# The wide products of two feed-forwards and a short convolution: high weights against both token parts in one matmul

## The chip, the cores and the metric

The kernel runs on one core of a Trainium2 chip. The metric is the device time of one launch in microseconds; the profile's span is counted from the first to the last instruction of one such execution, inside that time. An engine's name in a row is PE (TensorE matmul), PEld (TensorE weight load), DVE (VectorE), ACT (ScalarE), POOL (GpSimd) or SP (SyncE, whose queue issues the loads).

## The reference

One token block of 256 rows and 1024 columns goes through a feed-forward, a token mixing (retention and neighbourhood attention), a second feed-forward, a recurrent mixer and a short-convolution mixer, all in float32. The stages that matter here:

```python
def _swiglu(x, w_in, w_out):                      # w_in 1024 x 5632, w_out 2816 x 1024
    g, u = jnp.split(x @ w_in, 2, axis=-1)
    return (jax.nn.silu(g) * u) @ w_out

def shortconv_mixer(h, w_in, conv_w, w_out):      # w_in 1024 x 6144, w_out 1536 x 1024
    u = jnp.einsum('bsd,dc->bsc', h, w_in)
    bg, cg = u[..., :WIDTH], u[..., WIDTH:2 * WIDTH]
    xv, gate = u[..., 2 * WIDTH:3 * WIDTH], u[..., 3 * WIDTH:]
    y = bg * causal_depthwise_conv(cg * xv, conv_w)
    return jnp.einsum('bsc,cd->bsd', y * jax.nn.silu(gate), w_out)
```

Each stage begins with an RMS norm of the running sum `x` and ends by adding its result to it.

## The kernel before, in words

**Products.** A float32 product is made of three matmuls in fp32r. Weights and tokens are each split in a high part (a rounded copy, by ACT, L94 for weights) and a low part (the rest, by DVE, L96); `mm3` (L240 to L244) passes high by high (L242), low by high (L243 or L244 by the operands' order) and high by low. The third low by low is dropped.

**Weights.** All weights come in parts of 128 x 1024 in one order, through the class `Stream`. A ring of 41 slots of 128 x 1024 (`RING`, L23) holds raw parts, their high and low halves, and the token pairs. `load` issues a part's DMA on SP's queue, `split` makes its halves, `use` (called at a part's first use) keeps the split up to 15 parts ahead as far as free slots less `S.reserve` allow, and `done` gives two slots back. So how far the weights run ahead is set by the ring.

**Token pairs.** `Pair` holds the transposed tokens: `h` and `l` tiles of four blocks of 128 x 256 each, in the ring. `transpose_pair` (L366 to L378) turns 128 x 128 blocks on PE (L372) and writes high by ACT (L376), low by DVE (L377).

**Stage one, `phase_a`** (from L431): columns of the weights come out on the partitions, tokens on the free side. The first unit or two of each stage are done per token half (`mm_tok`, tokens stationary, 512 weight columns moving). They begin before the second half of the tokens is there: `nxt.ready(1)` turns it in between. All other units, 256 weight columns and two parts each, go through `mm_a2`: for each 128 columns `m` and each of 8 blocks `k`, three matmuls with the weights stationary and 256 token columns moving (L242 high weights by high tokens, L243 high weights by low tokens, L244 low weights by high tokens), into half a PSUM bank. There are 8 banks, given out in rotation. In `ffn` the eviction `evac` (L499 to L509) holds the bank of the gate, and at the second of two units does silu on ACT (L505), the product on DVE (L506) and `split_pair` (L483, L484). In `shortconv` four units are held, then copied, multiplied, convolved and split (L1095 to L1106).

**Stage two, `phase_b`** (from L391): tokens stationary, 512 weight columns moving, two banks for each token half. The last 8 parts are passed first for one token half, so that the norm of this half runs while PE passes the other.

**The joint** between a stage two and the next stage one is where PE can run short: norm, transposes and weight splits share ACT and DVE. While a stage two runs, `S.reserve` is 4, so that the next token pair finds its slots; it is set to 0 once the pair is there.

The instructions of each engine are ordered by a scheduler which the program runs through when it is built; each engine then takes its own in order.

Of the kernel before, what the change touches and what calls it, by code (L numbers as in the profile page):

```python
# [19 lines left out]
RD = 128  # L20
NH, ND = 8, 64
EPS = 1e-6
RING = 41  # L23
RAW_AHEAD = 4
AHEAD = 15
RATE = 3
# [24 lines left out]
class Stream:  # L51
# [80 lines left out]
def block_kernel(ctx: ExitStack, tc: tile.TileContext, A, C, out):  # L132
# [4 lines left out]
    const = ctx.enter_context(tc.tile_pool(name="const", bufs=1))  # L137
    gp = ctx.enter_context(tc.tile_pool(name="gains", bufs=2))
    wp = ctx.enter_context(tc.tile_pool(name="work", bufs=2))
    tp = ctx.enter_context(tc.tile_pool(name="tmp", bufs=6))  # L140
# [60 lines left out]
    u_ax = ax  # L201
# [30 lines left out]
    one = const.tile([128, 128], F32, name="one")  # L232
    dve.memset(one, 1.0)
    S.ahead = 6
    S.load(4)
# [10 lines left out]
    class Pair:  # L246
# [27 lines left out]
        def drop(self):  # L274
            self.used(self.nk - 1)

    def mm_a2(bk, u, xt):

        for m in range(2):
            c = slice(m * 128, (m + 1) * 128)  # L280
            for q, p in enumerate(u.parts):
                if m == 0:
                    S.use(p)
                for j in range(p.a):
                    k = q * p.a + j
                    mm3(bk[:, m * SEQ:(m + 1) * SEQ], (p.hi[:, j, c], p.lo[:, j, c]), xt.at(k),
                        k == 0, k == u.a - 1)
                if m == 1:
                    S.done(p)

    def mm_tok(ps, u, q, xt, t):

# [87 lines left out]
    class Next:  # L380
# [5 lines left out]

        def ready(self, t):
            if self.pair is None:
                self.pair = Pair(NKD)
            S.hold = transpose_pair(self.hn[t], t, self.pair, 0, NKD)  # L390

    def phase_b(us, xt, post_ap, halved, next_ap, late, last=False):


        acc = [columns(0, 512, D), columns(0, 512, 768, D) if last else columns(0, 512, D)]
        ps = [p for u in us for p in u.parts]
        n, late = len(ps), 2 * late
        S.reserve = 4
        nxt = Next()
        for k, p in enumerate(ps[:n - late]):  # L400
            S.use(p)
            for t in range(2):
                mm_b(acc[t], p, xt, t, k, n)
            S.done(p)
            xt.used(k)
        post = gain(post_ap) if post_ap is not None else None
        pre = gain(next_ap)


        order = []  # L410
        for t in range(2):
            order += [(t, k, acc[t]) for k in range(n - late, n - 4)]
            order += [(t, k, [a]) for a in acc[t] for k in range(n - 4, n)]
        for q, (t, k, a) in enumerate(order):
            p = ps[k]
            if q == len(order) - 6 and not last:
                nxt.ready(0)
                S.reserve = 0
            if a[0] is acc[t][0]:
                S.use(p, 1 if t == 0 or last or nxt.pair else 0)  # L420
            mm_b(a, p, xt, t, k, n)
# [9 lines left out]
    def phase_a(tok, us, nxt, evac, tok_evac, lead):  # L431

# [27 lines left out]
                turned()  # L460
            turned = tok_evac(i, b)
        for i, u in enumerate(us):
            b = bank()
            mm_a2(b, u, xt)
            if turned:
                turned()
                turned = None
            evac(i, b)
# [25 lines left out]
    def ffn(us, nxt, post, next_ap, lead, aside=None):  # L494
        f = Pair(NKF)
        held = {}
        done = 2 * len(us[0])

        def evac(i, b):  # L499
            if i % 2 == 0:  # L500
                held[i] = b
                return
            g = held.pop(i - 1)
            sg = tmp()
            act.activation(out=sg, in_=g, func=AF.Silu)  # L505
            dve.tensor_tensor(out=sg, in0=sg, in1=b, op=ALU.mult)  # L506
            split_pair(f, done + i - 1, 2, two(sg))
            if done + i == 15 and aside:
                aside()  # L509
# [9 lines left out]
        xt = phase_a(us[0], us[1], nxt, evac, tok_evac, lead)  # L519
        xt.drop()  # L520
        return phase_b(us[2], f, post, True, next_ap, LATE_B)


# [30 lines left out]
    def mixing(nxt):  # L554
# [62 lines left out]


        nqk = [S.slot(F32, "nqk") for _ in range(2)]

        def full_a(u, xt):
            b = bank()
            mm_a2(b, u, xt)
            return b

        for i, u in enumerate(u_nq + u_nk):
            b = full_a(u, xt)
# [211 lines left out]
        for i, u in enumerate(u_gn + u_gr):  # L839
# [11 lines left out]
            elif i < 6:  # L851
                transpose_pair(yn[i - 4], i - 4, zt, 0, NKD)
                S.drop()
        xt.drop()


        for i, u in enumerate(u_no):
# [30 lines left out]
    vec_b = const.tile([128, 36], F32, name="vec_b")  # L888
    cneg = const.tile([128, 24], F32, name="cneg")

    def channel_vectors():
        r = tmp()
# [4 lines left out]
        S.fetch(r[0:36, 128:256], A["b_conv_w_2"].rearrange("k (h p) -> (k h) p", p=128))  # L897
        ps = bank()
        pe.transpose(ps[:, 0:96], r[0:96, 0:128], ident[0:96, 0:96])
        pe.transpose(ps[:, 96:132], r[0:36, 128:256], ident[0:36, 0:36])  # L900
# [12 lines left out]
    def recurrent(nxt):  # L913
# [139 lines left out]
                S.drop()  # L1053

        banks = []
        xt = phase_a(u_at, u_ax, nxt, evac, tok_evac, 1)

        for j, u in enumerate(u_ag):
            b = bank()
# [5 lines left out]
        xt.drop()  # L1065
        S.aside()
        for j in range(EARLY, 6):
            finish(j)
# [3 lines left out]
    def shortconv(nxt):  # L1072
# [21 lines left out]

        def evac(i, b):  # L1095
            held.append(b)
            if i % 4 != 3:
                return
            cg, xv, bg, gt = held
            held.clear()  # L1100
            w = tmp()
            act.activation(out=w, in_=cg, func=AF.Copy)
            dve.tensor_tensor(out=w, in0=w, in1=xv, op=ALU.mult)
            sg = tmp()
            act.activation(out=sg, in_=gt, func=AF.Silu)
            convolved(1 + i // 4, w, (bg, sg))  # L1106

        def tok_evac(i, b):
            w = tmp()
# [14 lines left out]
                    convolved(0, a, (g,))  # L1124
            return turned

        xt = phase_a(u_bt, u_b, nxt, evac, tok_evac, 2)
        xt.drop()
        return phase_b(u_bo, y, None, False, A["final_g_2"], LATE_B, last=True)


    LATE_B, LATE_O = 4, 3

    def prepare():
        S.fetch(rot, C["rot"])
        S.fetch(mask, C["mask"])
        decay_logs()
        channel_vectors()

    first = Next()  # L1140

# [76 lines left out]
```

## Time and profile before

| what | us |
| --- | --- |
| median of 3 runs | 922.97 (922.52 to 924.29) |
| the profiled execution: its own time | 922.03 |
| its span | 920.2 |
| PE busy in the span | 908.0 (99%) |
| DVE busy | 564.4 (61%) |
| ACT busy | 471.3 (51%) |

A matmul's busy time in a row is longer than the distance to the next one, since matmuls are pipelined and their ends are modelled. What a matmul costs is therefore read as the distance from one start to the next. Busy shares of ACT and DVE are averages over the stages; for a stage the windows are read.

### The profile page before, as it was taken

What the parts mean: (1) busy time and instruction counts of PE and PEld (TensorE: products, weight loads), DVE (VectorE), ACT (ScalarE), POOL (GpSimd) and SP (SyncE); (2) the same over time, 40 slices, a digit from 0 to 9 for tenths busy, and PEclk for the clock granted to TensorE, in tenths of its full rate; (3) what the DMA queues carried; (4) which work ended last, traced back from release to release, by engine and by line L of the source; (5) the groups of instructions that cost most, each with busy time, mean ns of one, the idle gap of its engine ahead of it and who ended that gap; (6) DMA issues with size and microseconds to landing.
All of it is one profiled execution on the core that took longest, in us unless ns stands there. A gap on an engine that the chain in (4) does not pass through costs nothing.

```text
span 920.2 us, 15017 instructions
## 1 busy us (share of the span) xinstructions
PE 908.0 (99%) x6082; PEld 836.0 (91%) x6082; DVE 564.4 (61%) x743; ACT 471.3 (51%) x672; POOL 13.1 (1%) x24
## 2 busy tenths in 40 slices
PE   8999999999999999999999999999999999999997
PEld 5999998888978899998899999888998879999986
DVE  6954646358945454666874446526787977656523
ACT  7844545335755454534664444515869755444412
POOL 0000000000000000000000000000000000000000
PEclk9999999999999999999999999999999999999999
DMA  9965547748536353667565546756525757555401
GB/s 292 348 209 161 174 164 251 251 107 243 179 115 227 118 174 115 215 184 243 166 209 160 162 160 205 240 191 206 186 93 191 245 159 252 184 160 184 161 1 46
DMA packets 132811, 168.67 MB, mean 183 GB/s; under 512 B 12545, under 2 KB 112645, under 8 KB 132742
## 3 DMA queue, kind: packets, MB, share of 16 engines
q1 hardware_dynamic: 132308, 167.11, 56.9%
q8 instruction: 48, 0.79, 0.3%
q10 hardware_dynamic: 434, 0.59, 0.2%
q14 instruction: 21, 0.17, 0.1%
HBM read 166.64 MB, written 1.05 MB: 182 GB/s over the span
## 4 chain that ended last, share of the span: by engine, by line
PE 90%; ACT 4%; DVE 3%; DMA 1%; issue 1%; SPq 0%; POOL 0%; POOLq 0%; DVEq 0%; ACTq 0%
PE bank L242 29%; PE bank L243 28%; PE bank L244 28%; PE bank L372 1%; DVE lo L96 1%; DVE ri L1045 1%; PE bank L754 1%; PE bank L779 1%; ACT hi L94 1%; DMA raw<-in_b_w_in 1%; ACT ri L982 1%; ACT u L981 1%; PE bank L664 0%; ACT ri L960 0%; DMA x<-in_x 0%
## 5 line engine op out<-in xcount | busy, mean ns | idle before, releaser
L96 DVE TENSOR_TENSOR lo<-raw,hi 128x1024 fp32r<-128x1024 f32 (+1 forms) x304 | 360.1, 1209 | 137.1 <-ACT hi L94 75.2
L242 PE MATMUL bank<-ph,hi 128*128 128x256 f32 x1360 | 387.3, 285 | 0.0
L94 ACT ACTIVATE hi<-raw 128x1024 fp32r<-128x1024 f32 (+1 forms) x304 | 308.1, 1044 | 152.5 <-PE bank L244 72.8
L243 PE MATMUL bank<-pl,hi 128*128 128x256 f32 x1360 | 385.0, 283 | 0.0
L244 PE MATMUL bank<-ph,lo 128*128 128x256 f32 x1360 | 385.0, 283 | 0.0
L243 PEld LDWEIGHTS bank<-pl,hi 128*128 128x128 f32 x1360 | 261.0, 192 | 0.4
L242 PEld LDWEIGHTS bank<-ph,hi 128*128 128x128 f32 x1360 | 261.0, 192 | 0.3
L244 PEld LDWEIGHTS bank<-ph,lo 128*128 128x128 f32 x1360 | 261.0, 192 | 0.1
L242 PE MATMUL bank<-hi,ph 128*128 128x512 f32 (+1 forms) x540 | 208.8, 387 | 1.1 <-ACT ph L376 1.1
L243 PE MATMUL bank<-lo,ph 128*128 128x512 f32 (+1 forms) x540 | 206.5, 383 | 0.0
L244 PE MATMUL bank<-hi,pl 128*128 128x512 f32 (+1 forms) x540 | 205.2, 383 | 0.1
L242 PEld LDWEIGHTS bank<-hi,ph 128*128 128x128 f32 x540 | 101.9, 189 | 23.5 <-ACT ph L376 3.2
L244 PEld LDWEIGHTS bank<-hi,pl 128*128 128x128 f32 x540 | 101.7, 189 | 20.4 <-DVE pl L377 0.8
L243 PEld LDWEIGHTS bank<-lo,ph 128*128 128x128 f32 x540 | 102.0, 189 | 19.6 <-DVE lo L96 0.6
L483 ACT ACTIVATE ph<-tmp 128x512 fp32r<-128x512 f32 x28 | 17.6, 629 | 60.2 <-DVE tmp L506 48.7
L327 ACT ACTIVATE tmp<-x 128x512 f32<-128x512 f32 (+1 forms) x25 | 15.4, 614 | 39.8 <-DVE x L352 31.1
L506 DVE TENSOR_TENSOR tmp<-tmp,bank 128x512 f32<-128x512 f32 x19 | 13.0, 685 | 30.8 <-PE bank L244 30.8
L360 DVE TENSOR_TENSOR tmp<-bank,g 128x512 f32<-128x512 f32 x12 | 8.3, 692 | 36.0 <-ACT tmp L357 35.7
L357 ACT ACTIVATE tmp<-bank 128x512 f32<-128x512 f32 x12 | 7.2, 599 | 42.7 <-PE bank L244 42.4
L484 DVE TENSOR_TENSOR pl<-tmp,ph 128x512 fp32r<-128x512 f32 x28 | 19.1, 690 | 11.8 <-ACT ph L483 11.8
L377 DVE TENSOR_TENSOR pl<-bank,ph 128x512 fp32r<-128x512 f32 x24 | 16.0, 686 | 14.2 <-ACT ph L376 14.2
L319 POOL TENSOR_TENSOR small<-small,half 128x1 f32<-128x1 f32 x18 | 10.8, 601 | 802.2 <-DVE small L317 802.2
(146 smaller groups left out, 432.9 us busy)
## 6 DMA issues: line engine op xcount, KB each, us to landing
raw<-in_ffn_w_in SPq DMA_DIRECT2D x76, 512.0 KB, 5.2
raw<-in_w_mix_in SPq DMA_DIRECT2D x52, 512.0 KB, 4.0
raw<-in_ffn_w_out SPq DMA_DIRECT2D x44, 512.0 KB, 4.0
raw<-in_b_w_in SPq DMA_DIRECT2D x40, 512.0 KB, 4.6
raw<-in_a_w_in SPq DMA_DIRECT2D x20, 512.0 KB, 6.1
raw<-in_a_w_out SPq DMA_DIRECT2D x12, 512.0 KB, 4.4
raw<-in_b_w_out SPq DMA_DIRECT2D x12, 512.0 KB, 4.4
raw<-in_w_ret_out SPq DMA_DIRECT2D x8, 512.0 KB, 4.9
```

The lines of the kernel that those rows point to most:

```text
L94: self.copied = self.nc.scalar.activation(out=p.hi, in_=p.raw, func=AF.Copy)
L96: self.nc.vector.tensor_tensor(out=p.lo, in0=p.raw, in1=p.hi.bitcast(F32), op=ALU.subtract)
L242: pe.matmul(ps, a[0], b[0], start=first, stop=False)
L243: pe.matmul(ps, a[0], b[1], start=False, stop=False)
L244: pe.matmul(ps, a[1], b[0], start=False, stop=last)
L319: nc.gpsimd.tensor_tensor(out=r, in0=v, in1=half[:, 0:1], op=ALU.pow)
L327: sq = act.activation(out=tmp()[:, :c1 - c0], in_=x[:, t, c0:c1], func=AF.Square, scale=1.0 / 32, accum_out=ss[:, c:c + 1])
L372: pe.transpose(ps[:, j * 128:(j + 1) * 128], src[:, (b + j) * 128:(b + j + 1) * 128], ident)
L377: d = dve.tensor_tensor(out=lo, in0=pv, in1=h.bitcast(F32), op=ALU.subtract)
L483: act.activation(out=h, in_=src, func=AF.Copy)
L484: dve.tensor_tensor(out=lo, in0=src, in1=h.bitcast(F32), op=ALU.subtract)
L506: dve.tensor_tensor(out=sg, in0=sg, in1=b, op=ALU.mult)
```

## The change

The units of `phase_a` in both feed-forwards and in the short convolution (20, 18 and 20 units; not the units per token half, and none of the mixing or of the recurrent mixer) go through `wide` in place of `mm_a2`. The stage's tokens lie in a tile `xt` in which the high and the low part of a block stand side by side (`both(k)`: 512 columns). For each 128 weight columns, eight matmuls pass the high weights by these 512 columns into a whole bank; eight more pass the low weights by the 256 high columns into the first half of it. The bank is then summed into a tile in SBUF: ACT copies its second half, DVE adds the first.

```diff
-RING = 41
+RING = 37
...
+    xp = ctx.enter_context(tc.tile_pool(name="xt", bufs=1))
+    tp = ctx.enter_context(tc.tile_pool(name="tmp", bufs=7))
...
+    class Wide:
+        def __init__(self):
+            self.t = xp.tile([128, NKD, 2, SEQ], F32R, tag="x", name="xt")
...
+    def mm_a2w(bs, u, xt, after):
+        for m, b in enumerate(bs):
+            c = slice(m * 128, (m + 1) * 128)
+            for z in range(2):
+                for q, p in enumerate(u.parts):
+                    if m == z == 0:
+                        S.use(p)
+                    for j in range(p.a):
+                        k = q * p.a + j
+                        if z == 0:
+                            pe.matmul(b, p.hi[:, j, c], xt.both(k), start=k == 0, stop=False,
+                                      skip_group_check=True)
+                        else:
+                            pe.matmul(b[:, 0:SEQ], p.lo[:, j, c], xt.at(k)[0], start=False,
+                                      stop=k == u.a - 1, skip_group_check=True)
+                    if m == z == 1:
+                        S.done(p)
+            after(m, b)
+
+    def wide(u, xt, out):
+        def summed(m, b):
+            o = out[:, m * SEQ:(m + 1) * SEQ]
+            act.activation(out=o, in_=b[:, SEQ:], func=AF.Copy)
+            dve.tensor_tensor(out=o, in0=b[:, 0:SEQ], in1=o, op=ALU.add)
+        mm_a2w([bank(), bank()], u, xt, summed)
+        return out
...
-                self.pair = Pair(NKD)
+                self.pair = Wide()
...
-        S.reserve = 4
...
-                S.reserve = 0
...
-            b = bank()
-            mm_a2(b, u, xt)
+            b = product(u, xt)
```

All token tiles of a stage one are now `Wide`, with a place of their own, and the ring is shorter by the four slots which a pair took. `phase_b` no longer changes `S.reserve`: it stays 2 in the first feed-forward and at the joint after it, and 4 from the mixing's end to the recurrent mixer's. In `ffn` silu is done in place on the summed gate as soon as it is there, in `shortconv` the first product of two units at the second of them, and the copy L1102 is gone. Four small table fetches of the first stage are issued four units earlier than their use (`channel_fetch`).

On PE in the first feed-forward, in the middle of its `phase_a`, the row was a repeating triple (`ph`, `pl`: high and low tokens; `hi`, `lo`: weights):

```order
L242 MATMUL bank<-ph,hi 128x256
L243 MATMUL bank<-pl,hi 128x256
L244 MATMUL bank<-ph,lo 128x256
L242 MATMUL bank<-ph,hi 128x256
L243 MATMUL bank<-pl,hi 128x256
L244 MATMUL bank<-ph,lo 128x256
```

Now, at the same place:

```order
L305 MATMUL bank<-xt,hi 128x512 x8
L308 MATMUL bank<-xt,lo 128x256 x8
L305 MATMUL bank<-xt,hi 128x512 x8
L308 MATMUL bank<-xt,lo 128x256 x8
```

Twenty-four matmuls with a weight load each became sixteen, of the same 6144 columns in all.

On DVE at the same place, before (L506 is the gate's product, L484 the split of the result):

```order
L506 TENSOR_TENSOR tmp<-tmp,bank 128x512
L96 TENSOR_TENSOR lo<-raw,hi 128x1024
L484 TENSOR_TENSOR pl<-tmp,ph 128x512
L96 TENSOR_TENSOR lo<-raw,hi 128x1024 x5
L506 TENSOR_TENSOR tmp<-tmp,bank 128x512
```

Now (L319 the sum, L553 the gate's product, L532 the split of the result):

```order
L319 TENSOR_TENSOR tmp<-bank,tmp 128x256
L96 TENSOR_TENSOR lo<-raw,hi 128x1024
L553 TENSOR_TENSOR tmp<-tmp 128x512
L96 TENSOR_TENSOR lo<-raw,hi 128x1024
L319 TENSOR_TENSOR tmp<-bank,tmp 128x256
L96 TENSOR_TENSOR lo<-raw,hi 128x1024
L532 TENSOR_TENSOR pl<-tmp,ph 128x512
```

The sums stand between the splits, four for each two units.

On DVE at the joint between the mixing and the second feed-forward, before (L345 scales the second token half `hn`, L516 is the product of the first per-half unit, L377 the low part of the turned tokens):

```order
L333 TENSOR_TENSOR hn<-x,g 128x512
L317 TENSOR_SCALAR small<-small 128x1
L345 TENSOR_SCALAR hn<-hn,small 128x512 x2
L516 TENSOR_TENSOR tmp<-tmp,bank 128x256 x2
L377 TENSOR_TENSOR pl<-bank,ph 128x4x128 x2
L96 TENSOR_TENSOR lo<-raw,hi 128x1024 x7
```

Now, at the same joint:

```order
L384 TENSOR_TENSOR hn<-x,g 128x512 x2
L368 TENSOR_SCALAR small<-small 128x1
L563 TENSOR_TENSOR tmp<-tmp,bank 128x256
L396 TENSOR_SCALAR hn<-hn,small 128x512 x2
L428 TENSOR_TENSOR xt<-bank,xt 128x4x128 x2
L96 TENSOR_TENSOR lo<-raw,hi 128x1024 x7
```

The product of the per-half unit (L516, now L563) moved ahead of the scaling of `hn`, for which the transposes wait.

## Rows read from the trace of the kernel before

**Rows 1.** The page: busy times, PE's granted clock, and the chain that ended last

```profile
PE 908.0 (99%) x6082; PEld 836.0 (91%) x6082; DVE 564.4 (61%) x743; ACT 471.3 (51%) x672; POOL 13.1 (1%) x24
PEclk9999999999999999999999999999999999999999
PE 90%; ACT 4%; DVE 3%; DMA 1%; issue 1%; SPq 0%; POOL 0%; POOLq 0%; DVEq 0%; ACTq 0%
```

**Rows 2.** Windows over the three wide stages: busy us of each engine (instructions)

```profile
25.00:142.00 117.00, 117.00 (x966) 116.42 (x966) 71.55 (x104) 60.14 (x70) 0.00 (x0) 1.00 0.63 207
446.00:600.00 154.00, 153.75 (x1093) 145.08 (x1092) 91.26 (x89) 77.47 (x89) 0.00 (x0) 1.00 0.59 190
755.00:868.00 113.00, 113.00 (x905) 111.24 (x904) 71.64 (x84) 54.29 (x69) 0.00 (x0) 1.00 0.58 187
```

**Rows 3.** Timeline of PE, first feed-forward: start, duration, 256-column matmuls

```profile
59.82 0.28 PE L244 MATMUL bank<-ph,lo 128*128 128x256 f32 x1
59.94 0.28 PE L242 MATMUL bank<-ph,hi 128*128 128x256 f32 x1
...
61.50 0.28 PE L243 MATMUL bank<-pl,hi 128*128 128x256 f32 x1
```

**Rows 4.** Timeline of PE, last stage two: 512-column matmuls in a row

```profile
899.72 0.39 PE L244 MATMUL bank<-hi,pl 128*128 128x512 f32 x1
...
903.12 0.39 PE L244 MATMUL bank<-hi,pl 128*128 128x512 f32 x1
```

**Rows 5.** Timeline of PE there: three matmuls of 512 and six of 256, alternating

```profile
904.06 0.40 PE L242 MATMUL bank<-hi,ph 128*128 128x512 f32 x1
...
904.76 0.28 PE L242 MATMUL bank<-hi,ph 128*128 128x256 f32 x1
...
908.28 0.40 PE L242 MATMUL bank<-hi,ph 128*128 128x512 f32 x1
```

**Rows 6.** Groups by line and form: count, busy us, mean ns, idle before

```profile
L96 DVE TENSOR_TENSOR lo<-raw,hi 128x1024 fp32r<-128x1024 f32 x296 | 354.9, 1223 | 136.8 <-ACT hi L94 75.2 <-PE bank L243 40.8 <-issue 17.3
L94 ACT ACTIVATE hi<-raw 128x1024 fp32r<-128x1024 f32 x296 | 303.6, 1056 | 152.4 <-PE bank L244 72.8 <-PE bank L243 29.6 <-DVE lo L96 26.5
L783 ACT ACTIVATE tmp<-bank 128x256 f32<-128x256 f32 x8 | 3.0, 380 | 9.7 <-PE bank L779 9.7
L516 DVE TENSOR_TENSOR tmp<-tmp,bank 128x256 f32<-128x256 f32 x6 | 2.5, 419 | 2.6 <-ACT tmp L515 2.6
```

**Rows 7.** Waits of PEld, whole span: us in total, times, longest

```profile
PEld bank L242 <- ACT ph L376: 3.2, 8, 0.5
PEld bank L243 <- DVE lo L96: 0.6, 2, 0.4
```

**Rows 8.** Windows over the four joints, columns as in rows 2

```profile
200.00:216.00 16.00, 15.74 (x74) 12.70 (x73) 13.98 (x22) 8.74 (x15) 1.10 (x2) 1.00 0.70 114
446.00:452.00 6.00, 5.75 (x32) 4.69 (x31) 5.04 (x7) 5.38 (x9) 0.00 (x0) 1.00 0.07 14
622.00:636.00 14.00, 13.74 (x82) 11.64 (x81) 9.84 (x17) 8.23 (x16) 1.10 (x2) 1.00 0.73 226
720.00:750.00 30.00, 29.56 (x133) 24.00 (x132) 25.94 (x33) 17.70 (x25) 2.01 (x2) 1.00 0.74 241
```

**Rows 9.** Timeline, joint after the mixing: DVE, ACT and PE

```profile
443.33 0.88 DVE L345 TENSOR_SCALAR hn<-hn,small 128x512 f32<-128x512 f32 x2 [0.66 <-POOL small L319]
444.36 1.28 ACT L515 ACT_TABLE_LOAD   x1 [4.48 <-PE bank L244]
445.65 0.38 ACT L515 ACTIVATE tmp<-bank 128x256 f32<-128x256 f32 x1
446.39 1.04 PE L372 MATMUL bank<-ident,hn 128*128 128x128 f32 x8
```

**Rows 10.** Timeline of DVE, joint after the recurrent mixer

```profile
720.63 11.45 DVE L96 TENSOR_TENSOR lo<-raw,hi 128x1024 fp32r<-128x1024 f32 x10
```

More of the change, by code (lines that the diff above doesn't have):

```diff
@@ L139, in block_kernel @@
     wp = ctx.enter_context(tc.tile_pool(name="work", bufs=2))
-    tp = ctx.enter_context(tc.tile_pool(name="tmp", bufs=6))
+    xp = ctx.enter_context(tc.tile_pool(name="xt", bufs=1))
+    tp = ctx.enter_context(tc.tile_pool(name="tmp", bufs=7))
     sp = ctx.enter_context(tc.tile_pool(name="small", bufs=8))
@@ L231, in block_kernel @@
     nc.scalar.dma_start(out=ident, in_=C["ident"])
-    one = const.tile([128, 128], F32, name="one")
+    one = tp.tile([128, 512], F32, tag="t", name="one")[:, 0:128]
     dve.memset(one, 1.0)
@@ L275, in drop, with at, both, view @@
             self.used(self.nk - 1)
+    class Wide:
+        def __init__(self):
+            self.t = xp.tile([128, NKD, 2, SEQ], F32R, tag="x", name="xt")
+        def at(self, k, t0=0, t1=SEQ):
+            return self.t[:, k, 0, t0:t1], self.t[:, k, 1, t0:t1]
+        def both(self, k):
+            return self.t[:, k].rearrange("p z t -> p (z t)")
+        def view(self, part, k, n):
+            return self.t[:, k:k + n, part, :]
+    def mm_a2w(bs, u, xt, after):
[23 more added lines that the diff above has]
+        return out
     def mm_a2(bk, u, xt):
@@ L289, in mm_a2, with full_a @@
                     S.done(p)
+    def full_a(u, xt):
+        b = bank()
+        mm_a2(b, u, xt)
+        return b
     def mm_tok(ps, u, q, xt, t):
@@ L429, in phase_b, with phase_a @@
         return nxt
-    def phase_a(tok, us, nxt, evac, tok_evac, lead):
+    def phase_a(tok, us, nxt, evac, tok_evac, lead, product):
         xt = nxt.pair
@@ L501, in evac @@
                 held[i] = b
+                act.activation(out=b, in_=b, func=AF.Silu)
                 return
-            g = held.pop(i - 1)
-            sg = tmp()
-            act.activation(out=sg, in_=g, func=AF.Silu)
+            sg = held.pop(i - 1)
             dve.tensor_tensor(out=sg, in0=sg, in1=b, op=ALU.mult)
             split_pair(f, done + i - 1, 2, two(sg))
-            if done + i == 15 and aside:
-                aside()
+            if aside and done + i in (11, 15):
+                aside(done + i == 11)
         def tok_evac(i, b):
@@ L517, in tok_evac @@
             return lambda: split_pair(f, 2 * i, 2, two(turn_tok(sg)))
-        xt = phase_a(us[0], us[1], nxt, evac, tok_evac, lead)
-        xt.drop()
+        xt = phase_a(us[0], us[1], nxt, evac, tok_evac, lead, lambda u, xt: wide(u, xt, tmp()))
         return phase_b(us[2], f, post, True, next_ap, LATE_B)
@@ L619, in mixing @@
         nqk = [S.slot(F32, "nqk") for _ in range(2)]
[L621 to L624, printed above, removed]
         for i, u in enumerate(u_nq + u_nk):
@@ L853, in mixing @@
                 S.drop()
-        xt.drop()
         for i, u in enumerate(u_no):
@@ L889, in block_kernel, with channel_fetch @@
     cneg = const.tile([128, 24], F32, name="cneg")
-    def channel_vectors():
-        r = tmp()
+    def channel_fetch():
+        r = wp.tile([128, D], F32, tag="w", name="r")
         S.fetch(r[0:48, 0:128], A["a_conv_w_2"].rearrange("k (h p) -> (k h) p", p=128))
@@ L897, in channel_vectors @@
         S.fetch(r[0:36, 128:256], A["b_conv_w_2"].rearrange("k (h p) -> (k h) p", p=128))
+        return r
+    def channel_vectors(r):
         ps = bank()
@@ L1055, in recurrent @@
         banks = []
-        xt = phase_a(u_at, u_ax, nxt, evac, tok_evac, 1)
+        xt = phase_a(u_at, u_ax, nxt, evac, tok_evac, 1, full_a)
         for j, u in enumerate(u_ag):
@@ L1064, in recurrent @@
                 to_decay((3, 4, 5))
-        xt.drop()
         S.aside()
@@ L1096, in evac @@
             held.append(b)
+            if i % 4 == 1:
+                dve.tensor_tensor(out=held[0], in0=held[0], in1=b, op=ALU.mult)
             if i % 4 != 3:
@@ L1100, in evac @@
             held.clear()
[L1101 to L1106, printed above, removed]
+            act.activation(out=gt, in_=gt, func=AF.Silu)
+            convolved(1 + i // 4, cg, (bg, gt))
         def tok_evac(i, b):
@@ L1125, in tok_evac, with prepare @@
             return turned
-        xt = phase_a(u_bt, u_b, nxt, evac, tok_evac, 2)
-        xt.drop()
+        xt = phase_a(u_bt, u_b, nxt, evac, tok_evac, 2, lambda u, xt: wide(u, xt, tmp()))
         return phase_b(u_bo, y, None, False, A["final_g_2"], LATE_B, last=True)
     LATE_B, LATE_O = 4, 3
[L1134 to L1138, printed above, removed]
+    fetched = []
+    def prepare(early):
+        if early:
+            S.fetch(rot, C["rot"])
+            S.fetch(mask, C["mask"])
+            fetched.append(channel_fetch())
+        else:
+            decay_logs()
+            channel_vectors(fetched[0])
     first = Next()
```

## The prediction

> **What bounds the kernel now.** I read the page first: PE is busy in 99% of the span, its granted clock is at the upper level (2.4 GHz) in all 40 slices, and 90% of the chain that ended last is PE [rows 1]. Next the windows over the three stages that the change touches, to see whether this average holds there: PE is busy in all of 384 us but 0.25, DVE in 59 to 63% and ACT in 48 to 51% [rows 2]. So the time there is PE's column stream, and what a matmul costs is what counts. A busy PE says little of that, since busy times overlap; I took start-to-start distances from the timeline instead. In the first feed-forward fourteen 256-column matmuls go from 59.82 to 61.50: 120.0 ns each [rows 3]. In the last stage two, fifteen of 512 columns go from 899.72 to 903.12: 226.7 ns each [rows 4]. Last I looked at the waits: in the whole span the weight loads waited 0.6 us for split weights and 3.2 us for turned tokens [rows 7]; PE is hardly ever short of work.
>
> **What the change removes on PE.** The two distances differ by 106.7 ns for 256 columns, that is 0.417 ns a column (one column each cycle of 2.4 GHz); what is left is the same in both, 226.7 - 213.3 = 120.0 - 106.7 = 13.3 ns, a fixed cost of one matmul with its weight load. The columns stay: a triple had 3 x 256, a pair now has 512 + 256. One matmul and one load of each triple go, so a triple of 3 x 120.0 = 360.0 ns becomes 226.7 + 120.0 = 346.7 ns. The units are 20 + 18 + 20 = 58, each with 2 x 8 = 16 triples: 928 triples x 13.3 ns = **12.4 us less**.
>
> All of it lies on the path, as PE has no idle time in these stages to absorb it [rows 2].
>
> The Trainium skill, TensorE: Matmul & The Clock Gate, section Back-to-back issue gap, gives the distance of single warm matmuls as columns over 2.4 GHz plus about 2.5 ns. By that a removed matmul would be worth 928 x 2.5 ns = 2.3 us, an estimate from that page of the Trainium skill. The trace disagrees: 120.0 and 226.7 ns have a fixed part five times as large.
>
> **What it adds on PE.** Matmuls of 512 and of 256 columns now alternate in blocks of eight. The last stage two shows such a mix, three of 512 and six of 256: the three take 0.70 us from 904.06 to 904.76 in place of 0.68, and three whole rounds to 908.28 take 4.22 us in place of 3 x (3 x 226.7 + 6 x 120.0) = 4.20 [rows 5]. So one round of both sizes costs about 7 ns extra. There are 116 such rounds (58 units x 2): **0.8 us more**. Bounds: nothing, or the 20 ns of the three wide ones alone, 2.3 us.
>
> **What it adds on ACT and DVE.** Each unit gets two copies of 128 x 256 from PSUM (nearest row: 380 ns on ACT) and two sums (nearest row: 419 ns on DVE) [rows 6]. For the 20 units of the first feed-forward that is 40 x 0.38 = 15.2 us on ACT and 40 x 0.42 = 16.8 us on DVE. DVE then has 71.6 + 16.8 = 88.4 us in some 113 us, 78%, ACT 75.3 of 113, 67%. In the short convolution it is the same 16.8 us on 71.6 in some 109 us, 81%; the lost copies L1102 are not needed for the argument. PE waits for a sum only through its bank: a bank is filled in 8 x 346.7 ns = 2.8 us, and the next in the rotation of eight comes up some 20 us later. So the cost on the path is nothing while DVE stays under 100%. What would be late next if it did not is the splits, which share both engines: ACT's largest idle time before a split is 72.8 + 29.6 us of waiting for PE, and 26.5 us for DVE [rows 6]. That is a ring full of split weights, so there is slack to spend in the middle of a stage. The silu in place and the products from SBUF have the form and place of what they replace; I take them at nothing.
>
> **What it moves: the joints.** There are two parts to this. First, order. After the mixing, DVE's scaling of the second token half now stands behind the product of the first per-half unit, which waits for silu and its table load on ACT. In the trace this scaling began at 443.33 and PE came to the transposes only at 446.39 [rows 9]. By the new order six matmuls of the per-half pass come behind the transposes, so PE gets there 6 x 0.227 = 1.4 us earlier, at 445.0. Twelve matmuls stand between the first unit's end and the transposes, so ACT can start its table load at 445.0 - 2.7 = 442.3; 1.28 + 0.38 + 0.42 us later, at 444.4, the scaling starts, and 0.45 us later the first half is there: 444.9. That is just in time; I allow 0.3 us. Second, depth. The ring has four slots less and the tokens take none, so where the reserve was 4 during stage two and is now 2 (first joint) the weights lose two slots, one part; at the other three joints the reserve stays 4 and they lose four slots, two parts. PE lost 0.26, 0.25, 0.26 and 0.44 us of busy time at these joints [rows 8]. Since DVE made ten splits in 11.45 us after the recurrent mixer [rows 10] while PE uses a part in 2.7 to 2.9 us (twelve matmuls of 512 or twenty-four of 256), a lost part is soon made good. I take 0.5 us for all joints together. Below, they could give 0.5 us back, as there are fewer splits ahead of the additions to `x` after the recurrent mixer; above, see the third rival. The earlier table fetches and the place of the small tiles I take at nothing: none of the waits of rows 7 is theirs.
>
> **The sum.** The profiled execution took 922.03 us: 922.03 - 12.4 + 0.8 + 0.5 = 910.9. The median of the runs shown is 0.94 us above it, so I expect a median of **911.9 us**, 1.2% less.
>
> **Rival 1: the wide matmul saves almost nothing.** The 512 columns with weights stationary might cost as much as two matmuls of 256, 240 ns, as if the 13.3 ns went with the columns. Then only the additions are left: 922.97 + 0.8 + 0.5 = 924.3 us, within 0.2% of before. Rows 4 speak against it: there 512 columns with a load each take 226.7 ns. What rows 4 do not show is weights in the stationary place with 512 token columns; hence a small chance, 0.03. By the estimate from the Trainium skill's page (TensorE: Matmul & The Clock Gate, section Back-to-back issue gap) the time would be 924.3 - 2.3 = 922.0 us.
>
> **Rival 2: some joints run dry.** The lost depth shows in PE at one or two joints, with two or three parts split just in time: a split is 1.06 us on ACT and then 1.22 us on DVE, 2.3 us [rows 6], so three cost 6.9 us in place of the 0.5 taken: 918.3 us. For it: after the recurrent mixer DVE is busy for 25.9 of 30 us [rows 8]. Against: even there PE lost 0.44 us, and the scheduler can put matmuls of the other token half ahead. Chance 0.10.
>
> **Rival 3: slower, all joints dry.** The same mechanism at its full price: one part at the first joint and two at each of the others, seven parts in all, 7 x 2.28 = 16.0 us [rows 6]. That gives 922.97 - 12.4 + 0.8 + 16.0 = 927.4 us, slower by 0.5%. The point from which it decides: more than 11.6 us lost, that is at least five of the seven parts split with PE idle for the whole of it, without the next part being made meanwhile. Against it stand the 0.6 us of waits for split weights [rows 7]. Chance 0.03.
>
> **How the numbers follow.** My forecast has 0.84, the rivals 0.03, 0.10 and 0.03. The range: its low end takes the additions at nothing and the joints' gain, 922.97 - 12.4 - 0.5 = 910.1, less the 0.5 us by which the runs before lie under their median; the high end takes the alternation at 2.3 us and one dry joint (two parts, 4.6 us), 922.97 - 12.4 + 2.3 + 4.6 = 917.5, of which I keep 916.5 as both bounds at once are unlikely. What is left out are parts of rival 2 and rivals 1 and 3. A measurement of this kernel tells 0.2% (1.8 us) from no change; so faster 0.94 (forecast and rival 2), same 0.03 (rival 1), slower 0.03 (rival 3).
>
> **What would show it.** In the changed profile, L305 should stand at 226.7 ns from start to start and L308 at 120.0, with 928 rows of each and 5154 matmuls in all. The windows over the three stages should still show PE busy throughout, in about 4.3, 3.8 and 4.3 us less each, with DVE near 80%. L318 should take about 380 ns and L319 about 420. The joints should lose under 1 us each. I would be wrong if L305 stood at 235 ns or more, if PE's loads waited for `lo` for more than 3 us, or if a bank's sum ended a wait of PE.

## The result, and the profile after

The changed kernel takes **908.26 us** (median, 907.87 to 908.85), the kernel before 923.04 us beside it: ratio 0.984, 95% interval 0.982 to 0.986, 14.8 us less. Faster, as forecast, but the time lies 1.3 us below the low end of the range (909.6) and 3.6 us below the predicted 911.9. The profiled execution took 908.18 us against 922.03, a gain of 13.85 us where the sum had 11.1.

The page of the changed kernel: busy times, PE's granted clock, and the chain that ended last by engine, as in [rows 1].

```profile
PE 894.0 (99%) x5154; PEld 778.2 (86%) x5154; DVE 604.2 (67%) x859; ACT 503.8 (56%) x783; POOL 15.5 (2%) x24
PEclk9999999999999999999999999999999999999999
PE 97%; DVE 1%; ACT 1%; issue 0%; SPq 0%; DMA 0%; POOL 0%; POOLq 0%
```

PE has 928 matmuls less and is still the bound. Span less PE's busy time is 12.4 us, before it was 12.2: head, joints and tail together neither gained nor lost. The windows over the three wide stages, for [rows 2] (the stages now end earlier, so the bounds of the second and third have moved, and the first takes in some 3 us more of what follows):

```profile
25.00:142.00 117.00, 117.00 (x670) 101.69 (x669) 88.38 (x147) 74.85 (x113) 0.00 (x0) 1.00 0.67 213
441.00:592.00 151.00, 150.75 (x808) 129.07 (x807) 103.22 (x125) 88.00 (x124) 0.00 (x0) 1.00 0.60 190
742.00:854.00 112.00, 112.00 (x635) 97.01 (x634) 89.39 (x124) 68.69 (x105) 0.00 (x0) 1.00 0.58 190
```

PE is busy throughout, as before. DVE is at 76% and 80% in the first and the last of them, where 78% and 81% were forecast. The groups of the two new matmuls and of the eviction, which show that ACT idled for the bank (70.1 us in all) and not the bank for ACT:

```profile
L305 PE MATMUL bank<-xt,hi 128*128 128x512 f32 x928 | 235.3, 395 | 0.0
L308 PE MATMUL bank<-xt,lo 128*128 128x256 f32 x928 | 125.4, 277 | 0.0
L318 ACT ACTIVATE tmp<-bank 128x256 f32<-128x256 f32 x116 | 43.8, 377 | 70.8 <-PE bank L308 70.1
L319 DVE TENSOR_TENSOR tmp<-bank,tmp 128x256 f32<-128x256 f32 x116 | 48.9, 421 | 47.6 <-ACT tmp L318 47.5
```

377 and 421 ns answer to the 380 and 419 ns taken from [rows 6]. Next the timeline of PE in the first feed-forward, eight high and eight low matmuls to a round:

```profile
58.70 2.02 PE L305 MATMUL bank<-xt,hi 128*128 128x512 f32 x8
60.56 1.07 PE L308 MATMUL bank<-xt,lo 128*128 128x256 f32 x8
61.47 2.02 PE L305 MATMUL bank<-xt,hi 128*128 128x512 f32 x8
...
100.30 2.02 PE L305 MATMUL bank<-xt,hi 128*128 128x512 f32 x8
```

From 58.70 to 100.30 there are fifteen rounds of 2.773 us, or 346.7 ns for a pair: the forecast to the digit. But its parts are others: 61.47 - 60.56 gives 114 ns for a low matmul (forecast 120.0), 60.56 - 58.70 gives 233 ns for a high one (226.7). A 256-column matmul at 114 ns does not fit a cost of 120.0 ns for each [rows 3]. So I looked at products that the change does not touch. In the mixing they still have the three narrow matmuls, but their tokens now lie in `xt` too; those of the attention outputs still lie in a `Pair` in the ring (`ph`, `pl`):

```profile
343.99 0.28 PE L243 MATMUL bank<-xt,hi 128*128 128x256 f32 x1
...
347.39 0.28 PE L243 MATMUL bank<-xt,hi 128*128 128x256 f32 x1
...
379.67 0.28 PE L243 MATMUL bank<-ph,hi 128*128 128x256 f32 x1
...
383.27 0.28 PE L243 MATMUL bank<-ph,hi 128*128 128x256 f32 x1
```

Thirty matmuls take 3.40 us with tokens in `xt`, 113.3 ns each; thirty take 3.60 us with tokens in the ring, 120.0 ns each as before. Same code, same shape, same clock (1.00): what differs in the rows is the place of the tokens. Landmarks point the same way. The mixing and the recurrent stage, forecast at no change, are 1.6 and 1.5 us shorter from the transposes of the first token half at one joint to those at the next; by the second half's transposes it is 1.5 and 0.6 us.

**Theory 1**: the place of the token tile changes what a matmul costs, and this is the gain that the prediction lacks. **Rival**: the fixed cost of 13.3 ns belongs to every matmul, and the extra gain comes from order or depth of the ring. Under theory 1 there is a further question: what about the place counts, the halves side by side, the tile outside the ring, or its byte address against that of the weights? As allocated when the program is built, each ring buffer of the kernels before and after begins, within its partition, 128 bytes past a multiple of 256; `xt` begins 64 past one. Weight and token blocks are multiples of 512 and 1,024 bytes apart, so this difference of minus 64 holds for every matmul. In a `Pair` it is 0.

### The profile page after: what moved, and what is told of

Read it like the earlier page. It is cut to its first block, busy times and chain, and to the rows that moved or that the text cites. A ratio compares the mean times of both kernels' runs of the same rounds, so it can differ in the third digit from the quotient of the medians.

```text
span 906.4 us, 13302 instructions
## 1 busy us (share of the span) xinstructions
PE 894.0 (99%) x5154; PEld 778.2 (86%) x5154; DVE 604.2 (67%) x859; ACT 503.8 (56%) x783; POOL 15.5 (2%) x24
## 4 chain that ended last, share of the span: by engine, by line
PE 97%; DVE 1%; ACT 1%; issue 0%; SPq 0%; DMA 0%; POOL 0%; POOLq 0%
PE bank L305 24%; PE bank L243 19%; PE bank L244 19%; PE bank L245 18%; PE bank L308 12%; PE bank L988 1%; PE bank L423 1%; PE bank L795 1%; PE bank L820 1%; PE bank L705 0%; PE bank L780 0%; PE bank L524 0%; PE bank L684 0%; ACT xt L427 0%; DMA raw<-in_ffn_w_in 0%
## 5 line engine op out<-in xcount | busy, mean ns | idle before, releaser
L305 PE MATMUL bank<-xt,hi 128*128 128x512 f32 x928 | 235.3, 395 | 0.0
L305 PEld LDWEIGHTS bank<-xt,hi 128*128 128x128 f32 x928 | 166.0, 188 | 31.3
L308 PEld LDWEIGHTS bank<-xt,lo 128*128 128x128 f32 x928 | 123.4, 188 | 10.5
L308 PE MATMUL bank<-xt,lo 128*128 128x256 f32 x928 | 125.4, 277 | 0.0
L245 PE MATMUL bank<-hi,pl 128*128 128x512 f32 (+1 forms) x316 | 120.5, 382 | 0.0
L244 PE MATMUL bank<-lo,ph 128*128 128x512 f32 (+1 forms) x316 | 120.4, 382 | 0.0
L243 PE MATMUL bank<-hi,ph 128*128 128x512 f32 (+1 forms) x316 | 120.3, 381 | 0.0
L243 PE MATMUL bank<-xt,hi 128*128 128x256 f32 x336 | 95.5, 284 | 0.0
L244 PE MATMUL bank<-xt,hi 128*128 128x256 f32 x336 | 93.5, 278 | 0.0
L245 PE MATMUL bank<-xt,lo 128*128 128x256 f32 x336 | 93.5, 278 | 0.0
L243 PE MATMUL bank<-hi,xt 128*128 128x512 f32 (+1 forms) x224 | 88.7, 398 | 1.2 <-ACT xt L427 0.8
L244 PE MATMUL bank<-lo,xt 128*128 128x512 f32 (+1 forms) x224 | 87.1, 391 | 0.0
L245 PE MATMUL bank<-hi,xt 128*128 128x512 f32 (+1 forms) x224 | 85.6, 389 | 0.0
L318 ACT ACTIVATE tmp<-bank 128x256 f32<-128x256 f32 x116 | 43.8, 377 | 70.8 <-PE bank L308 70.1
L319 DVE TENSOR_TENSOR tmp<-bank,tmp 128x256 f32<-128x256 f32 x116 | 48.9, 421 | 47.6 <-ACT tmp L318 47.5
L243 PEld LDWEIGHTS bank<-hi,ph 128*128 128x128 f32 x316 | 59.4, 188 | 11.4
L243 PEld LDWEIGHTS bank<-xt,hi 128*128 128x128 f32 x336 | 63.4, 189 | 0.2
L244 PEld LDWEIGHTS bank<-xt,hi 128*128 128x128 f32 x336 | 63.3, 188 | 0.2
```

The source lines that it names most:

```text
L243: pe.matmul(ps, a[0], b[0], start=first, stop=False)
L244: pe.matmul(ps, a[0], b[1], start=False, stop=False)
L245: pe.matmul(ps, a[1], b[0], start=False, stop=last)
L305: pe.matmul(b, p.hi[:, j, c], xt.both(k), start=k == 0, stop=False, skip_group_check=True)
L308: pe.matmul(b[:, 0:SEQ], p.lo[:, j, c], xt.at(k)[0], start=False, stop=k == u.a - 1, skip_group_check=True)
L318: act.activation(out=o, in_=b[:, SEQ:], func=AF.Copy)
```

## The experiments

**1. The place alone.** The changed kernel with all products narrow again and the evictions of before; the tile `xt` and 37 ring buffers stay.

```diff
-        xt = phase_a(us[0], us[1], nxt, evac, tok_evac, lead, lambda u, xt: wide(u, xt, tmp()))
+        xt = phase_a(us[0], us[1], nxt, evac, tok_evac, lead, full_a)
...
-        xt = phase_a(u_bt, u_b, nxt, evac, tok_evac, 2, lambda u, xt: wide(u, xt, tmp()))
+        xt = phase_a(u_bt, u_b, nxt, evac, tok_evac, 2, full_a)
```

> The changed kernel with every product back in three 256-column matmuls and the evictions of before; only the place of the token tile is kept: one tile of its own, high and low halves of a block side by side, 37 ring buffers. Theory 1 (the place or layout of the tokens sets part of the fixed cost of a matmul): 1,264 triples, those of the wide stages and those of the mixing and recurrent stages, fall from 360.0 ns to 340 to 353 ns (113.3 to 117.8 ns a matmul), so 898 to 915 us. Rival (the place is irrelevant, and only the number of columns counts): every matmul of these stages is at 120.0 ns and the time is that of the kernel before, 922 to 924 us. Theory 1 with the gain tied to stages that the wide product does not touch would show 120.0 ns in the feed-forward stages and 113 to 118 ns in the mixing.

Measured: **903.52 us**, ratio 0.979 (0.977 to 0.981): faster than the changed kernel, without the wide product. The page's busy times and PE's timeline in the first feed-forward:

```profile
PE 888.6 (99%) x6082; PEld 814.7 (90%) x6082; DVE 562.7 (62%) x743; ACT 468.9 (52%) x672; POOL 15.5 (2%) x24
```
```profile
59.80 0.28 PE L243 MATMUL bank<-xt,hi 128*128 128x256 f32 x1
...
69.66 0.28 PE L243 MATMUL bank<-xt,hi 128*128 128x256 f32 x1
```

87 matmuls in 9.86 us, 113.3 ns each; 340 ns a triple against 346.7 for the wide pair at this place. So 13.3 ns do not belong to every matmul; what the shorter ring does by itself, run 10 shows.

**2. Alternating.** High and low matmul alternate block by block.

```diff
+                    pe.matmul(b, p.hi[:, j, c], xt.both(k), start=k == 0, stop=False,
+                              skip_group_check=True)
+                    pe.matmul(b[:, 0:SEQ], p.lo[:, j, c], xt.at(k)[0], start=False,
+                              stop=k == u.a - 1, skip_group_check=True)
```

> The changed kernel with the high 512-column matmul and the low 256-column matmul alternating block by block instead of eight of the one and then eight of the other. If a change between the two widths costs nothing in itself: 346.7 ns for a pair still, 908 us. If each change costs the 7 ns that the prediction took from the alternation in the kernel before: 14 more changes for each 8 pairs, 116 times, so 116 x 14 x 7 ns = 11.4 us more, about 919 to 920 us.

Measured: 914.37 us, 6.1 us more than the changed kernel, between the two. A pair takes 353.3 ns (235 and 118), 6.7 ns more than in rows of eight: 928 x 6.7 ns = 6.2 us, or 3.8 ns for each of the 14 added changes in a round. Changes of width do cost; eight in a row is the better order.

**3. Wide everywhere.** Also nq, nk, gn, gr of the mixing, and the recurrent units.

```diff
-            b = full_a(u, xt)
+            b = wide(u, xt, tmp())
...
-        xt = phase_a(u_at, u_ax, nxt, evac, tok_evac, 1, full_a)
+        xt = phase_a(u_at, u_ax, nxt, evac, tok_evac, 1, lambda u, xt: wide(u, xt, tmp()))
```

> The changed kernel with the wide product also in the mixing stage (nq, nk, gn, gr) and for the recurrent units: 18 more units, 288 more triples. Theory 1 (their three narrow matmuls already run at 113.3 to 117.8 ns, 340 to 353 ns a triple, against 346.7 ns for a wide pair): minus 2 to plus 2 us, so 906 to 910 us. Rival (a fixed cost of 13.3 ns for every matmul and load, as the prediction had it): 288 x 13.3 ns = 3.8 us less, 904.4 us.

Measured: 914.44 us, 6.2 us more than the changed kernel; both expectations missed. Windows over the recurrent stage, the changed kernel first, then this one, and its waits of PE (us in total, times, longest):

```profile
645.00:715.00 70.00, 68.56 (x481) 63.95 (x480) 61.06 (x95) 59.62 (x100) 0.00 (x0) 1.00 0.43 143
```
```profile
645.00:715.00 70.00, 63.95 (x374) 56.38 (x374) 57.22 (x94) 57.11 (x101) 0.00 (x0) 0.95 0.35 116
```
```profile
PE bank L988 <- DVE u L1018: 3.6, 2, 3.4
PE bank L988 <- ACT u L1013: 2.4, 1, 2.4
```

PE lost 4.6 us more of this stage: its waits at the gate matmuls (L988) are 6.0 us, in the changed kernel 1.4. These matmuls need the short convolution `u` of each unit, which now starts only behind the two evictions; that this is why it comes late is read from the program and was not tested. The windows differ in the granted clock too, 1.00 against 0.95. From the end of each of the two longest waits (2.4 and 3.4 us) it stands at its lower level (0.50, 1.2 GHz) for 3.4 us:

```profile
650.50:653.90 3.40, 3.29 (x8) 2.67 (x9) 3.40 (x5) 3.37 (x5) 0.00 (x0) 0.50 0.06 13
684.70:688.10 3.40, 3.03 (x10) 2.70 (x11) 3.40 (x7) 0.47 (x1) 0.00 (x0) 0.50 0.00 0
```

At half the clock 6.8 us do the work of 3.4, so 3.4 us are lost. Together 4.6 + 3.4 = 8.0 us, an estimate, where the two profiled executions differ by 8.1 (916.24 and 908.18). So the waits and the clock decided here, and not the distance between matmuls, which the expectations were about.

**4. The halves apart.** As run 1, high and low tokens in two tiles.

```diff
-            self.t = xp.tile([128, NKD, 2, SEQ], F32R, tag="x", name="xt")
+            self.t = [xp.tile([128, NKD, SEQ], F32R, tag=f"x{z}", name="xt") for z in range(2)]
```

> As the run with only the place of the tokens kept, but with high and low tokens in two separate tiles, so that the halves of a block do not lie side by side. If the side-by-side halves are what makes a matmul cheaper: 120.0 ns again and 922 to 924 us. If a place outside the ring is what does it (another offset against the weights): 113 to 118 ns as in the run with one tile, and its time.

Measured: 904.29 us, 113.3 ns in most stretches and 117.8 in others. Lying side by side is not the cause.

**5. Shifts by stage, narrow.** As run 1, the tile 512 bytes longer and used from `o` on; shifts in elements of 4 bytes.

```diff
+    SHIFT = [16, 16, 8, 16, 32]
...
+            o = SHIFT.pop(0)
+            t = xp.tile([128, NKD * 2 * SEQ + 128], F32R, tag="x", name="xt")
+            self.t = t[:, o:o + NKD * 2 * SEQ].rearrange("p (k z t) -> p k z t", k=NKD, z=2)
```

> As the run with only the place of the tokens kept (113.3 ns a matmul in the two feed-forwards and the short convolution, 903.5 us), but with the token tile shifted inside a larger one, by another amount in each stage: 64 bytes in the first feed-forward, the mixing and the recurrent stage, 32 bytes in the second feed-forward, 128 bytes in the short convolution. The ring buffers begin 128 bytes past a multiple of 512, the token tile 64 bytes past one. Theory A (alignment in the low address bits against the weights decides, modulo 128 bytes): after 64 bytes the tokens stand to the weights as in the ring, so 120.0 ns in the first feed-forward and the mixing, 113.3 ns after 128 bytes. Theory B (lying outside the ring decides, whatever the alignment): 113 to 118 ns in every stage and 902 to 907 us.

Measured: 919.9 us, one execution; the distances below are what counts. PE's timeline in the first feed-forward, the second, and the short convolution:

```profile
59.92 0.28 PE L243 MATMUL bank<-xt,hi 128*128 128x256 f32 x1
...
70.00 0.28 PE L243 MATMUL bank<-xt,hi 128*128 128x256 f32 x1
...
499.97 0.28 PE L243 MATMUL bank<-xt,hi 128*128 128x256 f32 x1
...
509.91 0.28 PE L243 MATMUL bank<-xt,hi 128*128 128x256 f32 x1
...
809.81 0.28 PE L243 MATMUL bank<-xt,hi 128*128 128x256 f32 x1
...
819.71 0.28 PE L243 MATMUL bank<-xt,hi 128*128 128x256 f32 x1
```

84 matmuls each: 10.08, 9.94 and 9.90 us, so 120.0, 118.3 and 117.9 ns. Moving the tile by 64 bytes brings 120.0 ns back, in the mixing and the recurrent stage too. Theory B is out. Theory A holds for the 64 bytes but not in its period: after 128 bytes the 113.3 ns did not return.

**6 and 7. The ring moved by 64 bytes**, in the kernel before (run 6) and in run 1 (run 7).

```diff
+    pad = ctx.enter_context(tc.tile_pool(name="pad", bufs=1))
+    pad.tile([128, 16], F32, name="pad")
     ring = ctx.enter_context(tc.tile_pool(name="ring", bufs=RING))
```

> The kernel before with 64 unused bytes in front of the ring, so that weights and tokens are shifted together: they stand to each other as before, but begin 192 bytes past a multiple of 512, not 128. If only the position of tokens and weights to each other counts: 120.0 ns and 922 to 924 us. If the alignment of each by itself counts (a start at an odd multiple of 64 bytes is the better one): 113 to 118 ns, up to 1,292 triples x 20 ns = 26 us less, 897 to 915 us.

> The run with only the place of the tokens kept, with 64 unused bytes in front of the ring: weights 192 and tokens 128 bytes past a multiple of 512 (there 128 and 64). If only the position of the two to each other counts: 113 to 118 ns and 902 to 906 us, as there. If the tokens' own start at an odd multiple of 64 bytes is what counts: 120.0 ns and 922 to 924 us.

Measured: 922.72 us, ratio 1.000 (0.999 to 1.001), 120.0 ns; and 902.52 us, ratio 0.978 (0.976 to 0.979), 113.3 or 117.8 ns. The first feed-forward, run 6 and then run 7, thirty matmuls each:

```profile
59.84 0.28 PE L246 MATMUL bank<-ph,lo 128*128 128x256 f32 x1
...
63.44 0.28 PE L246 MATMUL bank<-ph,lo 128*128 128x256 f32 x1
```
```profile
59.74 0.28 PE L245 MATMUL bank<-xt,hi 128*128 128x256 f32 x1
...
63.14 0.28 PE L245 MATMUL bank<-xt,hi 128*128 128x256 f32 x1
```

The address of each by itself does not count, the difference does.

**8. Shifts by stage, wide.** The changed kernel with the edit of run 5.

> The changed kernel with the same shifts of the token tile by stage: 64 bytes in the first feed-forward, the mixing and the recurrent stage, 32 bytes in the second feed-forward, 128 bytes in the short convolution. If the alignment of tokens to weights sets a fixed cost for wide matmuls too: eight high and eight low ones take something else than 2.773 us in the first feed-forward (2.77 us again after 128 bytes). If a wide matmul does not depend on it: 2.77 us in all three stages, 906 to 910 us.

Measured: 912.85 us, one execution. A round takes 2.793 us at difference 0, 2.813 at minus 32, and 2.741 and 2.773 by turns at plus 64, against 2.773 at minus 64. A wide pair depends on the difference too, by less.

**9 and 10. Two by two.** Shifted by 64 bytes in every stage, so that the difference is 0 as in the ring: wide (run 9) and narrow (run 10).

```diff
-    SHIFT = [16, 16, 8, 16, 32]
+    SHIFT = [16, 16, 16, 16, 16]
```

> The changed kernel with its token tile shifted by 64 bytes in every stage, so that tokens stand to the weights as they did in the ring: the wide product alone, without the new place. With 2.793 us for eight pairs (the first feed-forward of the run with shifts by stage) 928 pairs take 349.2 ns against 360.0 ns for three narrow ones: 10.0 us less than the kernel before, 912 to 914 us. If the wide product had gained nothing of its own and the place all: 922 to 924 us; by the prediction's 13.3 ns for each pair: 910 to 911 us.

> Three narrow matmuls everywhere, and the token tile of its own shifted by 64 bytes in every stage: neither the wide product nor the new alignment, only the tile of its own and 37 ring buffers are left. If alignment is the whole of the effect of the place: 120.0 ns in all stages and 922 to 924 us, the time of the kernel before. If the tile of its own or the smaller ring has a part of its own: another time at 120.0 ns.

Measured: 911.95 us, ratio 0.988 (0.987 to 0.989), and 922.33 us, ratio 0.999 (0.998 to 1.000).

| median, us | difference 0, as in the ring | minus 64 |
| --- | --- | --- |
| three narrow matmuls | 922.33 (run 10) | 903.52 (run 1) |
| wide pair | 911.95 (run 9) | 908.26 (the change) |

In the row of the wide pair, too, the 336 triples of the mixing and the recurrent stage are narrow and change with the column.

The timeline of run 9, with rounds of 2.793 us (seven from 57.72 to 77.27, of which 1.84 us are high matmuls):

```profile
57.72 2.00 PE L309 MATMUL bank<-xt,hi 128*128 128x512 f32 x8
59.56 1.11 PE L312 MATMUL bank<-xt,lo 128*128 128x256 f32 x8
60.51 2.00 PE L309 MATMUL bank<-xt,hi 128*128 128x512 f32 x8
...
77.27 2.00 PE L309 MATMUL bank<-xt,hi 128*128 128x512 f32 x8
```

In run 10 thirty matmuls of the first feed-forward take 3.60 us again, 120.0 ns each:

```profile
59.79 0.28 PE L244 MATMUL bank<-xt,hi 128*128 128x256 f32 x1
...
63.39 0.28 PE L244 MATMUL bank<-xt,hi 128*128 128x256 f32 x1
```

Run 10 is within 0.7 us of the kernel before: the tile of its own and the smaller ring have no effect that counts.

**11. More shifts**, narrow: `SHIFT = [48, 4, 24, 64, 80]` in run 5.

> Three narrow matmuls everywhere, with other shifts of the token tile: tokens stand to the weights, modulo 512 bytes, at plus 128 in the first feed-forward, minus 48 in the mixing, plus 32 in the second feed-forward, plus 192 in the recurrent stage, plus 256 in the short convolution. So far 0 gave 120.0 ns, minus 32 118.7, minus 64 113.3 or 117.7, plus 64 117.7. If the pattern repeats every 128 bytes: 120.0 ns at plus 128 and plus 256, 113 to 118 ns at plus 192, 118.7 ns at plus 32. If it repeats only at 512 bytes or not at all: other values at plus 128, plus 192 and plus 256.

Measured: 917.83 us, one execution. Means of a 256-column matmul over the undisturbed part of each stage, with those of runs 1 and 5, by the difference tokens less weights modulo 256:

| difference, bytes | ns a matmul | run |
| --- | --- | --- |
| 0 | 120.0 | 5; 11 at plus 256 |
| plus 32, 64, 128 | 116.7, 117.8, 118.7 | 11, 5, 11 |
| minus 64 | 113.3 or 117.8 | 1; 11 at plus 192 |
| minus 48, minus 32 | 119.1, 118.3 | 11, 5 |

Plus 256 is again 120.0 and plus 192 again 113.3 or 117.8, and plus 128 is not 120.0: as far as these shifts go, the pattern repeats at 256 bytes, neither at 128 nor only at 512.

**12. In the ring itself.** The kernel before, with tokens of narrow products 192 bytes into a longer ring buffer (38 buffers).

```diff
-            return self.ring.tile([128, 1024], dt, tag="s4", name=name)
+            return self.ring.tile([128, 1088], dt, tag="s4", name=name)[:, o:o + 1024]
...
-                self.pair = Pair(NKD)
+                self.pair = Pair(NKD, 48)
-        zt = Pair(NKD)
-        ot = Pair(4)
+        zt = Pair(NKD, 48)
+        ot = Pair(4, 48)
```

> The kernel before, its tokens still in the ring and its products still three narrow matmuls. Ring buffers are 4,352 bytes long (17 times 256), 38 in place of 41, and those that hold tokens for a narrow product are used from byte 192 on, so that these tokens stand 64 bytes short of the weights modulo 256, as the changed kernel's tile does. The tokens of the wide-column halves stay where they were. If this alignment is the whole effect of the place: 113.3 or 117.7 ns for all 1,360 narrow triples, the 96 of the attention outputs too, 900 to 906 us. If a tile outside the ring is needed as well: 120.0 ns and 922 to 924 us.

Measured: 906.47 us (904.77 to 908.62), ratio 0.982 (0.981 to 0.984), half a microsecond above the range expected. PE's timeline in the first feed-forward:

```profile
59.92 0.28 PE L243 MATMUL bank<-pl,hi 128*128 128x256 f32 x1
...
69.78 0.28 PE L243 MATMUL bank<-pl,hi 128*128 128x256 f32 x1
```

87 matmuls at 113.3 ns with tokens in the ring; the products of the attention outputs, 120.0 ns in every other run, are at 117.8. The difference in address is enough by itself. This kernel is 3 us behind run 1, the profiled executions 3.8 (906.47 and 902.70). In its trace PE is idle for 15.2 us of the span against 12.2, and the granted clock stands at 0.50 for 3.4 us from 14.6 and again from 683.6, the second time as PE waits 2.6 us for the short convolution of the recurrent stage; run 1 has no such stretch before its end. Why the waits are longer was not tested.

## Why the prediction was right in direction and short in size

- **The wide product: right, for the place it was read at.** Run 9 against run 10 has it alone: 10.4 us less. The terms were 12.4 us less for the matmuls and 0.8 more for the alternation. Measured at difference 0, a pair takes 349.2 ns against 360.0: 10.8 x 928 = 10.0 us. The 2.5 ns a pair over the forecast are 20 ns a round of eight and eight, the upper bound that the prediction gave the alternation, not the 7 ns it took: 2.3 us, not 0.8. They stand behind the switch: in the first feed-forward of run 9 the first five high matmuls of a row take 236, 236, 228, 232 and 231 ns on the mean, the last three 226.7 as forecast. That run 9 lands on the predicted 911.9 is partly luck: the sum had 11.1 us less, run 9 has 11.0, but as 10.0 from the pairs, 0.7 that run 10 has without them, and 0.4 not assigned. In the changed kernel the pair stands at 346.7 ns by another sum (233 and 114 ns), an agreement that says nothing for the terms.
- **The step that failed: "What the change removes on PE" took 13.3 ns as "a fixed cost of one matmul with its weight load", wherever the tokens lie, and "What it moves" priced of their new place only the slots of the ring.** The 13.3 ns are the cost of tokens and weights at difference 0, the only one in the trace before. At minus 64 a narrow matmul has 113.3 - 106.7 = 6.7 ns, while a wide one takes about 233 ns, more than at 0; so the split into columns and one fixed cost does not hold there. And the 336 unchanged triples of the mixing and recurrent stages, costed at nothing, became cheaper. From run 9 to the changed kernel, all start-to-start distances of matmuls with tokens of `xt` moving sum to 448.38 and 442.54 us, 5.8 us less: 2.0 of it are the wide pairs (low matmuls 4.6 less, high ones 2.6 more), 3.8 the narrow triples. Those with `xt` stationary rose by 1.9 us (512 columns at 229 to 230 ns instead of 227 to 228). Together 3.9 us less; the medians differ by 3.7, which is what the predicted 911.9 was short by.
- **Evictions: right.** 377 and 421 ns, DVE at 76% and 80% in the full windows, and no wait of a PE matmul for a sum is among the profile's waits.
- **Joints: right in size.** All of PE's idle time went from 12.2 to 12.4 us, where 0.5 us was allowed. At the joint after the mixing the scaling of the second token half is in time but for 0.34 us of the weight loads' waiting (0.3 forecast, [rows 9]); DVE, weight loads and the table load there:

```profile
438.20 1.28 ACT L562 ACT_TABLE_LOAD   x1
440.25 0.88 DVE L396 TENSOR_SCALAR hn<-hn,small 128x512 f32<-128x512 f32 x2
440.78 0.86 PEld L423 LDWEIGHTS bank<-ident,hn 128*128 128x128 f32 x8 [0.34 <-DVE hn L396]
```

- **The rivals** fell as argued: no joint ran dry (2 and 3), and the wide matmul saves at difference 0 (1). But at minus 64 rival 1 holds in a worse form: the wide pair costs 346.7 ns against 340 for three narrow ones, and the changed kernel is 4.7 us slower than run 1, which keeps only the tile (928 x 6.7 ns would be 6.2). One slip in rival 3 changes nothing: five parts of 2.28 us are 11.4, short of the 11.6 from which it decides, so it needed six. The version that beats both kernels is run 1 or 7: about 20 us, 2.1 to 2.2%, less than before, with the plain three matmuls.
- **The sign that was missed.** The prediction asked for L305 at 226.7 and L308 at 120.0 ns; they came at 233 and 114. Only their sum fitted. A check that names the parts shows this, one that names the sum does not.

## What to carry to other kernels

A start-to-start distance read from a trace holds for the operands' addresses there; a change that moves a tile changes it also for the products whose code it leaves alone, so list every matmul that reads the moved tile. Before matmuls are merged to save their fixed cost, try where moving and stationary operand begin modulo 256 bytes: here 64 bytes of padding were worth nearly twice the merge. Test a gain by undoing its parts one by one, since the part that the change is named for is worth 10 us by itself, the place 19 us by itself, and at the better place the first is a loss.

## What the runs showed of the hardware

- The distance of 256-column float32r matmuls, each with its own weight load, depends on the start of the moving operand less that of the stationary one modulo 256 bytes: 120.0 ns at 0, 113.3 or 117.8 at minus 64, others between (table of run 11; granted clock 1.00). With both moved by 64 bytes it stayed at 120.0 ns (run 6).
- 512-column matmuls prefer the opposite: with tokens stationary 227 to 228 ns at 0, 229 to 230 at minus 64, about 233 at minus 32 and plus 64 (runs 5 and 1). In one stage of the changed kernel minus 64 gave 231.5.
- The Trainium skill, SBUF — State Buffer, section SBUF: two separate sides, says that on the engines' side only the port pair shared by VectorE and GpSimd makes anyone wait. Runs 1 and 10, which differ in a shift of the token tile by 64 bytes, show PE's pace change with the addresses of its own two operands (113.3 and 120.0 ns in the first feed-forward); whether PE waits at the memory for that, no run here shows.
- The Trainium skill, TensorE: Matmul & The Clock Gate, section Back-to-back issue gap, gives 2.5 ns over the columns for an isolated matmul. The least here is 6.7 ns (113.3 - 106.7), but of matmuls in rows, each with its weight load; a matmul by itself no run here shows.
- The granted clock fell to 0.50 for 3.4 us at the end of each of PE's waits of 2.4 and 3.4 us in run 3. Eight 512-column matmuls that began at 652.09, in the first of these stretches, took 2.91 us from start to start of their rows; those from 655.91, at 1.00, took 1.86.
- Open: why one and the same difference of minus 64 gives 113.3 ns in one stretch and 117.8 in another, each constant for many matmuls. The tile's place is the same in both, and the same stretch (the first feed-forward from about 102 us on) has 113.3 in run 1 and 117.8 in run 7; no run tells what sets it.
